# Projecting the low-rank inputs before the shift is known, and adding the shift's nine columns afterwards

## The chip, the cores and the metric

The kernel runs on one core of a Trainium2 chip. The metric is the device time of one execution in microseconds: 1757.57 us, the median of three runs (1754.29 to 1759.15). The five engines are named as the profile names them: PE (TensorE, with PEld for its weight loads), DVE (VectorE), ACT (ScalarE), POOL (GpSimd) and SP (SyncE), which issues nearly all DMA transfers.

## The reference, cut to what matters

One layer of an encoder is computed for 384 tokens: 128 sample tokens (8 sequences of 16) and 256 tokens of one prompt. Only its beginning is touched here.

```python
mod = silu(c) @ w_ada + b_ada              # 9 sequences, 6 x 1024 columns
sh1, sc1, g1, sh2, sc2, g2 = split(mod, 6)
h = rmsnorm(x, norm1_w) * (1 + sc1) + sh1  # sc1, sh1: one row per sequence
P = h @ w_in                               # split into P_rw, P_dsa, P_gate
X = P_rw + (P_prev - P_rw) * mu_rw         # P_prev: the token before
r, k, v, wd, ad, gd = split(X, [1024, 1024, 1024, 64, 64, 160])
w_log = -softplus(-(w0 + tanh(wd) @ w_up)) - 0.5
a = sigmoid(a0 + ad @ a_up)
g = sigmoid(gd) @ g_up
```

The low-rank inputs are the last 288 columns of the RWKV part of `w_in`: wd, ad and gd.

## The kernel before

**Layout.** Activations are kept transposed: `xT` holds 8 chunks of 128 features by 384 tokens, tokens 0 to 127 being the sample. A projection takes its weights as high and low halves (an fp32r copy by ACT, L230, and the remainder by DVE, L234) and the activations likewise (`LTh`, `LTl`). Each chunk then needs three products of 128x384: high x high, low x high, high x low. `tposp` adds 24 of them into one PSUM bank.

**The front, in program order.** `front_x` loads x in three tiles of 128 tokens, normalises them and transposes them into `xT`. `front_h` walks over four pairs of feature chunks. For each pair it calls `mod_unit` twice: a unit loads 256 columns of `w_ada` as two tiles of 512 KB (L240), multiplies them with the nine conditioning rows (products `mm<-w,cst`), copies the result out (`mr`, L391) and turns it into columns with two tiny products (`bx<-cfirst,mr`); DVE adds the bias into `scT` (L396). Units 0 to 3 are the shift, units 4 to 7 the scale. Before, they come in the order 0, 4, 1, 5, 2, 6, 3, 7. Then `h1A` (scale times norm weight) is formed, `xT` is multiplied and shifted, and `LTh` and `LTl` of the pair are written.

**After the front.** `shifted("wa")`, `shifted("wb")` and `shifted("wg")` in `rwkv_head` project the low-rank inputs (units of 128, 128 and 96 columns of `w_in`) with `tposp`, copy them into `pt` and mix each token with the token before it. Then the string `ORDER` sets the sequence of all further units: it starts with two gate units G0 and G1 and the indexer, and goes on with gate units, RWKV pairs, attention quarters and the other 16 modulation units.

**What sets the order of the work.** Nothing is placed by hand at this place. Each engine runs its instructions strictly in the order that the compiler's scheduler gave it, and waits where an input is missing. All 512 KB weight tiles, of `w_ada` and `w_in` alike, share one ring `w` of four buffers (`raw`, L240): SP can ask for the next tile only when the instructions that read the tile four places earlier are done, and everything behind it in SP's queue waits with it. `issue_after` puts what is written in its block behind a named instruction. PSUM has eight banks in rings by tag: `mm` 2, `fx` 2, `dx` 2, `bx` 1, `cp` 1.

**Names around the change.** `tile_pool` objects are regions of SBUF: `ph` serves the front and is given back after it; `rw` and `idx` are opened later, in part on the same memory; `fconst` lives until the end of the RWKV part. `cfront` is a block of constants of 463 KB; DVE builds `expb` (L332) from it, POOL builds the rotary tables `rt` (L341 to L350) from `crope`.

Of the kernel before, what the change touches and what calls it, by code (L numbers as in the profile page):

```python
# [12 lines left out]
F32 = mybir.dt.float32  # L13
# [182 lines left out]
class K:  # L196
# [184 lines left out]
    def mod_unit(self, u):  # L381
# [5 lines left out]
        for h in (first, 1 - first):  # L387
            for g in range(4):
                self.mm(p[32 * g:32 * g + 32], self.st[:, h * 4 + g], w[h][:, g], start=(h == first), stop=(h != first), tp=(0, 32 * g))
        mr = self.t([128, 256], tag="mr", bufs=2, pool=self.fill)  # L390
        nc.scalar.activation(mr, p, AF.Copy)  # L391
        if u < 8:
            q = self.ps([128, 2, 9], tag="bx")
            for c in range(2):
                self.mm(q[:, c], mr[:, c * 128:(c + 1) * 128], self.c["sel"])
            nc.vector.tensor_tensor(self.scT[:, u // 4, (u % 4) * 2:(u % 4) * 2 + 2], q,  # L396
                                    self.bcol[:, 2 * u:2 * u + 2].unsqueeze(2).to_broadcast([128, 2, 9]), op=OP.add)
        else:
            nc.sync.dma_start(self.modd[:, u * 256:(u + 1) * 256], mr)

    def mod_cols(self, cs):
# [42 lines left out]
    def front_x(self):  # L444
# [3 lines left out]
        for i in range(3):  # L448
            x = self.t([128, 1024], tag="x", bufs=2)
            nc.sync.dma_start(x, self.I["x"][i * 128:(i + 1) * 128])  # L450
# [11 lines left out]
    def front_h(self):  # L462
# [6 lines left out]
        self.h1A = self.pool.tile([128, 8, 9], F32, name="h1A")  # L469
        h = self.xT  # L470
        for c in range(0, 8, 2):
            cs = slice(c, c + 2)
            self.mod_unit(c // 2)
            self.mod_unit(c // 2 + 4)
            self.mod_cols(cs)
            hs = h[:, cs, 0:128]
            o = hs.rearrange("p c (b t) -> p c b t", t=16)
            bc = lambda a: a[:, cs, :8].unsqueeze(3).to_broadcast([128, 2, 8, 16])
            nc.vector.tensor_tensor(o, o, bc(self.h1A), op=OP.mult)
            nc.vector.tensor_tensor(o, o, bc(self.h1B), op=OP.add)  # L480
            for cc in (c, c + 1):
# [4 lines left out]
            nc.vector.tensor_tensor(lo[:, cs, 0:128], hs, hi[:, cs, 0:128], op=OP.subtract)  # L486
            nc.gpsimd.tensor_tensor(lo[:, cs, 128:NT], h[:, cs, 128:NT], hi[:, cs, 128:NT], op=OP.subtract)  # L487


    def shifted(self, name, ch, tag, bufs=2):  # L490

        nc = self.nc
        W, m = self.win(name)
        pt = self.t([128, 393], tag="pt", bufs=2)
# [4 lines left out]
        nc.gpsimd.memset(ptp[:, 0:1], 0.0)  # L499
        p = self.tposp(W, 0, m, self.LT)  # L500
        nc.scalar.activation(pts[:, :, 1:], p[:, 0:128].rearrange("p (b t) -> p b t", t=16), AF.Copy)
        nc.scalar.activation(ptp[:, 1:], p[:, 128:NT], AF.Copy)
        Xs = X[:m, 0:128].rearrange("p (b t) -> p b t", t=16)
# [1092 lines left out]
    def run(self):  # L1596
        hs = self.ctx.enter_context(ExitStack())
        self.halves = self.open(hs, "halves")
        with ExitStack() as front:
# [6 lines left out]
            with ExitStack() as s:  # L1606
                self.pool = self.open(s, "ph")
                self.setup()
                self.mod_head()
                self.front_x()  # L1610
                self.front_h()

                self.early = {name: self.raw(self.win_ap(name)) for name in ("wa", "wb", "wg")}
                with self.tc.issue_after(self.wdma.ins):
                    self.load_consts("cfront", self.fconst)
                    self.setup_front()
# [145 lines left out]
```

## Time and profile before

| What | Value |
|---|---|
| three runs | 1754.29, 1757.57, 1759.15 us |
| profiled execution: time, span | 1749.86 us, 1748.1 us |
| busy share of the span | PE 96%, PEld 81%, DVE 78%, ACT 43%, POOL 32% |
| mean granted TensorE clock | 0.983 |
| chain of waits, by engine | PE 61%, DVE 18%, DMA 11%, issue 5%, ACT 3%, POOL 2% |
| PE idle in 0 to 60 us, from the windows view (60 less 43.85 busy) | 16.2 us |
| first product of a modulation unit | 10.96 us |
| first product of the low-rank inputs (wa) | 37.25 us |
| first product of wg | 50.26 us |
| first product of gate unit G0 | 54.54 us |

A row of the timeline reads: start in us, duration in us, engine, source line, operation, output tile <- input tiles, shape, count, and in brackets the idle time of the engine just before and what released it. A row of the windows view reads: stretch, its length, busy us of PE, PEld, DVE, ACT and POOL (with counts of instructions), the granted clock, the busy share of the DMA engines and GB/s. Rows of single products overlap, since matmuls are pipelined: the distance between two starts is what a product costs in a stream.

### The profile page before, as it was taken

How to read it: one execution, taken by the hardware profiler on the slowest of the kernel's cores; microseconds unless marked ns; L12 is line 12 of the kernel's file. 1: busy time of each engine (PE TensorE's matmuls, PEld its weight loads, DVE VectorE, ACT ScalarE, POOL GpSimd, SP SyncE). 2: the span in 40 equal slices, each digit the busy share in tenths (PEclk: the TensorE clock that was granted, in tenths of full speed). 3: DMA queues.
4: the chain of work that ended last, by engine and by line, in shares of the span. 5: the costliest groups of instructions: out<-in, count | busy, mean ns of one | idle time of the engine just before them, and what ended most of it. 6: DMA issues, size and time to landing. Idle time of an engine off the chain costs nothing.

```text
span 1748.1 us, 33136 instructions
## 1 busy us (share of the span) xinstructions
PE 1673.2 (96%) x12392; PEld 1410.4 (81%) x12392; DVE 1356.0 (78%) x2907; ACT 749.5 (43%) x1668; POOL 556.0 (32%) x621
## 2 busy tenths in 40 slices
PE   6999999999999988999998999999999999999998
PEld 4998788888878876999887899999966666767766
DVE  4448788878858855565999998999858777778787
ACT  4443333333343333444323365577843343343344
POOL 2434243343323310034032223431243324433242
PEclk8999899999999999999999999999999999999999
DMA  8543653465365366756398989986579999999996
GB/s 299 166 145 94 198 176 89 144 179 156 103 201 158 95 209 200 243 184 200 123 361 307 364 324 399 397 321 228 170 261 388 347 342 377 366 350 385 348 379 227
DMA packets 173049, 437.23 MB, mean 250 GB/s; under 512 B 46036, under 2 KB 86612, under 8 KB 156504
## 3 DMA queue, kind: packets, MB, share of 16 engines
q1 hardware_dynamic: 154456, 300.89, 50.8%
q0 software_dynamic: 18432, 134.23, 20.0%
q8 instruction: 98, 1.61, 0.4%
q14 instruction: 63, 0.52, 0.1%
HBM read 403.75 MB, written 31.30 MB: 249 GB/s over the span
## 4 chain that ended last, share of the span: by engine, by line
PE 61%; DVE 18%; DMA 11%; issue 5%; ACT 3%; POOL 2%; SPq 0%; DVEq 0%; POOLq 0%; ACTq 0%
PE mm L226 24%; PE fx L226 11%; PE dx L226 11%; PE cp L226 7%; PE bx L226 6%; DMA w<-in_pv 3%; DVE raw L1586 3%; DVE wl L234 3%; DVE acc L1592 3%; DMA raw<-in_puv,pe 2%; DMA w<-in_puT 1%; ACT wh L230 1%; DMA w<-in_w_in 1%; DMA w<-in_w_ada 1%; DVE psi L1321 1%
## 5 line engine op out<-in xcount | busy, mean ns | idle before, releaser
L234 DVE TENSOR_TENSOR wl<-w,wh 128x1024 fp32r<-128x1024 f32 (+1 forms) x276 | 346.9, 1264 | 116.5 <-ACT wh L230 78.4
L230 ACT ACTIVATE wh<-w 128x1024 fp32r<-128x1024 f32 (+1 forms) x284 | 297.0, 1051 | 167.2 <-PE mm L226 68.3
L1579 POOL DMA_INDIRECT raw<-in_puv,pe x128 | 175.5, 1371 | 419.8 <-PE dx L226 160.4
L226 PE MATMUL fx<-h2h,wl 128*128 128x256 f32 x704 | 199.6, 284 | 4.7 <-DVE wl L234 4.6
L226 PE MATMUL fx<-h2h,wh 128*128 128x256 f32 x704 | 200.7, 285 | 3.3 <-ACT wh L230 1.7
L226 PE MATMUL fx<-h2l,wh 128*128 128x256 f32 x704 | 197.3, 280 | 0.0
L1592 DVE SCALAR_TENSOR_TENSOR acc<-raw,dots,acc 128x1024 f32<-128x1024 f32 x127 | 166.1, 1308 | 13.7 <-ACT dots L1588 13.6
L1586 DVE SCALAR_TENSOR_TENSOR raw<-raw,sh 128x1024 f32<-128x1024 f32 x128 | 158.6, 1239 | 12.3 <-DMA raw<-in_puv,pe 12.2
L226 PEld LDWEIGHTS fx<-h2h,wh 128*128 128x128 f32 x704 | 132.8, 189 | 7.9 <-ACT wh L230 3.9
L226 PEld LDWEIGHTS fx<-h2h,wl 128*128 128x128 f32 x704 | 132.6, 189 | 7.9 <-DVE wl L234 7.1
L226 PEld LDWEIGHTS fx<-h2l,wh 128*128 128x128 f32 x704 | 132.9, 189 | 1.6 <-issue 1.1
L226 PE MATMUL mm<-LTh,wh 128*128 128x384 f32 (+2 forms) x352 | 124.0, 353 | 1.8 <-ACT wh L230 1.2
L226 PE MATMUL mm<-LTl,wh 128*128 128x384 f32 (+2 forms) x352 | 122.2, 347 | 1.2 <-POOL LTl L487 1.2
L226 PE MATMUL mm<-LTh,wl 128*128 128x384 f32 (+2 forms) x352 | 122.6, 348 | 0.0
L226 PE MATMUL mm<-h2f,w 128*128 128x256 f32 x448 | 105.5, 389 | 0.0
L226 PE MATMUL mm<-wh,LTh 128*128 128x256 f32 x336 | 99.3, 296 | 0.8 <-ACT qx L890 0.6
L226 PE MATMUL mm<-wl,LTh 128*128 128x256 f32 x336 | 100.0, 298 | 0.0
L226 PE MATMUL mm<-wh,LTl 128*128 128x256 f32 x336 | 98.8, 294 | 0.0
L1587 ACT ACTIVATE dots<-dots 128x1 f32<-128x1 f32 x128 | 25.5, 200 | 169.8 <-DVE raw L1586 169.2
L226 PEld LDWEIGHTS mm<-h2f,w 128*128 128x128 f32 x448 | 86.2, 195 | 12.6 <-issue 0.2
L226 PE MATMUL fx<-h2f,w 128*128 128x256 f32 x320 | 73.5, 382 | 0.0
L226 PEld LDWEIGHTS mm<-LTh,wh 128*128 128x128 f32 (+2 forms) x352 | 66.5, 189 | 7.3 <-ACT wh L230 2.1
(583 smaller groups left out, 4241.8 us busy)
## 6 DMA issues: line engine op xcount, KB each, us to landing
w<-in_puT SPq DMA_DIRECT2D x128, 512.0 KB, 6.2
w<-in_pv SPq DMA_DIRECT2D x128, 512.0 KB, 6.7
w<-in_w_in SPq DMA_DIRECT2D x70, 512.0 KB, 4.7
w<-in_w_ada SPq DMA_DIRECT2D x48, 512.0 KB, 4.9
cKT<-in_cKT SPq DMA_DIRECT2D x32, 256.0 KB, 4.4
cV<-in_cV SPq DMA_DIRECT2D x32, 256.0 KB, 4.0
w<-in_w_pq SPq DMA_DIRECT2D x16, 512.0 KB, 3.8
d<-wst SPq DMA_DIRECT2D x8, 832.0 KB, 4.3
```

The costliest lines, as they stand in the source:

```text
L226: return self.nc.tensor.matmul(out, l, r, start=start, stop=stop, skip_group_check=True, **kw)
L230: self.nc.scalar.activation(hi, src, AF.Copy)
L234: (self.nc.vector if eng == "v" else self.nc.gpsimd).tensor_tensor(lo, src, hi, op=OP.subtract)
L1321: nc.vector.max_index(si[:, half, h, 0:8], sv[:, half, h, 0:8], s[:, c])
L1579: d = nc.gpsimd.indirect_dma_start(out=bass.AP(tensor=u.tensor, offset=u.offset, ap=[u.ap[0], [1, 2048]]), out_offset=None, in_=self.I["puv"],
L1586: nc.vector.scalar_tensor_tensor(u, u, 1.0, h2, op0=OP.mult, op1=OP.mult, accum_out=dot)
L1587: nc.scalar.activation(dot, dot, AF.Gelu_apprx_tanh)
L1592: nc.vector.scalar_tensor_tensor(acc, v, dot, acc, op0=OP.mult, op1=OP.add)
```

## The change

1. `front_h` now runs the four scale units first (4, 5, 6, 7) and the four shift units after them (0, 1, 2, 3).
2. The low-rank weights wa, wb and wg get tiles of their own instead of places in the ring. They are loaded and split into halves behind the first scale unit, so ahead of 14 of the 16 tiles of `w_ada`.
3. After each scale unit the pair of chunks of x times scale is written as halves `EPh` and `EPl` (three ACT and three DVE instructions per pair), and the products of wa and wb with this pair are added into two `dx` banks. The 24 products of wg go into the `cp` bank, all behind the last product of the last shift unit.
4. After the last shift unit the nine shift columns are copied into a zeroed tile `z` (32 columns wide) and projected with the raw weights: 24 products into 32-row strips of a bank, one copy out (`shm`) and three small products that give `eshift` (128 x 9 for each of the three units).
5. `shifted` then reads the three banks directly and adds `eshift`: one DVE addition with a broadcast for the sample tokens, one ACT copy with a bias for the prompt.
6. `x` has three buffers instead of two; `shT` moves to another pool and is loaded ahead of `cfront`; the two ring places that were loaded ahead for wa and wb now hold G0 and G1.

```diff
@@ mod_unit
-                self.mm(p[32 * g:32 * g + 32], self.st[:, h * 4 + g], ...)
+                last = self.mm(p[32 * g:32 * g + 32], self.st[:, h * 4 + g], ...)
...
+        return last
@@ front_x
-            x = self.t([128, 1024], tag="x", bufs=2)
+            x = self.t([128, 1024], tag="x", bufs=3)
@@ front_h
+        eh, el = (self.t([128, 8, NT], F32R, tag=x) for x in ("EPh", "EPl"))
+        z = self.t([128, 8, 32], tag="shz")
+        nc.gpsimd.memset(z, 0.0)
+        names = ("wa", "wb", "wg")
+        self.ebank, W = {}, {}
+
+        def products(n, ks):
+            wh, wl, m, _ = W[n]
+            p = self.ebank[n][:m]
+            for k in ks:
+                self.mm(p, wh[:, k], eh[:, k], start=(k == 0), stop=False)
+                self.mm(p, wh[:, k], el[:, k], start=False, stop=False)
+                self.mm(p, wl[:, k], eh[:, k], start=False, stop=(k == 7))
+
         for c in range(0, 8, 2):
             cs = slice(c, c + 2)
-            self.mod_unit(c // 2)
             self.mod_unit(c // 2 + 4)
             self.mod_cols(cs)
+            if c == 0:
+                for n, tag in zip(names, ("dx", "dx", "cp")):
+                    m = UNITS[n][1]
+                    w = self.t([128, 8, m], tag=n)
+                    nc.sync.dma_start(w, self.win_ap(n))
+                    wh, wl = (self.t([128, 8, m], F32R, tag=n + x) for x in "hl")
+                    self.hilo(wh, wl, w)
+                    W[n] = wh, wl, m, w
+                    self.ebank[n] = self.ps([128, NT], tag=tag)
             hs = h[:, cs, 0:128]
             o = hs.rearrange("p c (b t) -> p c b t", t=16)
-            bc = lambda a: a[:, cs, :8].unsqueeze(3).to_broadcast([128, 2, 8, 16])
-            nc.vector.tensor_tensor(o, o, bc(self.h1A), op=OP.mult)
-            nc.vector.tensor_tensor(o, o, bc(self.h1B), op=OP.add)
+            nc.vector.tensor_tensor(o, o, self.h1A[:, cs, :8]..., op=OP.mult)
+            nc.scalar.activation(eh[:, cs, 0:128], hs, AF.Copy)
+            nc.vector.tensor_tensor(el[:, cs, 0:128], hs, eh[:, cs, 0:128], op=OP.subtract)
+            for cc in (c, c + 1):
+                hp, A = h[:, cc, 128:NT], self.h1A[:, cc, 8:9]
+                nc.scalar.activation(eh[:, cc, 128:NT], hp, AF.Identity, scale=A, bias=0.0)
+                nc.vector.scalar_tensor_tensor(el[:, cc, 128:NT], hp, A, eh[:, cc, 128:NT], ...)
+            for n in names[:2]:
+                products(n, (c, c + 1))
+        for c in range(0, 8, 2):
+            cs = slice(c, c + 2)
+            last = self.mod_unit(c // 2)
+            hs = h[:, cs, 0:128]
+            nc.vector.tensor_tensor(o, o, self.h1B[:, cs, :8]..., op=OP.add)
...
-
+        with self.tc.issue_after(last.ins):
+            products(names[2], range(8))
+
+        nc.vector.tensor_copy(z[:, :, 0:9], self.h1B)
+        p = self.ps([128, 352], tag="mm")
+        q = self.ps([128, 3, 9], tag="bx")
...
+        for i, n in enumerate(names):
+            _, _, m, w = W[n]
+            for h2 in range(2):
+                for g in range(4):
+                    k = h2 * 4 + g
+                    self.mm(p[32 * g:32 * g + 32, i * 128:i * 128 + m], z[:, k], w[:, k],
+                            start=(h2 == 0), stop=(h2 == 1), tp=(0, 32 * g))
+        nc.scalar.activation(mr, p, AF.Copy)
+        for i, n in enumerate(names):
+            m = W[n][2]
+            self.mm(q[:m, i], mr[:, i * 128:i * 128 + m], self.c["sel"])
+            nc.vector.tensor_copy(self.eshift[:m, i], q[:m, i])
@@ shifted
+        if early:
+            p, B = self.ebank[name][:m], self.eshift[:m, ch - 24]
+            nc.vector.tensor_tensor(pts[:, :, 1:], p[:, 0:128]..., B[:, 0:8]..., op=OP.add)
+            nc.scalar.activation(ptp[:, 1:], p[:, 128:NT], AF.Identity, scale=1.0, bias=B[:, 8:9])
@@ run
-                self.early = {name: self.raw(self.win_ap(name)) for name in ("wa", "wb", "wg")}
+                self.early = {name: self.raw(self.win_ap(name)) for name in ("G0", "G1")}
                 with self.tc.issue_after(self.wdma.ins):
+                    self.shT = self.fconst.tile([128, 8, 27], F32, name="shT")
+                    self.nc.sync.dma_start(self.shT, self.I["shT"])
```

Three places of the new order matter below. On PE, in the middle of the modulation units (`mm<-w,cst` are a unit's products, four to a row, `bx` its columns; `mm_277` is unit 6, `mm_316` unit 7 and `mm_355` unit 0 of the change). Before:

```order
L226 MATMUL mm_268<-w_269,cst 32x256 x4
L226 MATMUL mm_268<-w_271,cst 32x256 x4
L226 MATMUL mm_287<-w_288,cst 32x256 x4
L226 MATMUL bx_283<-cfirst,mr_281 128x9 x2
L226 MATMUL mm_287<-w_290,cst 32x256 x4
L226 MATMUL mm_315<-w_316,cst 32x256 x4
L226 MATMUL bx_302<-cfirst,mr_300 128x9 x2
L226 MATMUL mm_315<-w_318,cst 32x256 x4
```

Now:

```order
L226 MATMUL dx_211<-EPh_174,wbl_208 128x384
L226 MATMUL mm_277<-w_278,cst 32x256 x4
L226 MATMUL bx_253<-cfirst,mr_251 128x9 x2
L226 MATMUL mm_277<-w_280,cst 32x256 x4
L226 MATMUL mm_316<-w_317,cst 32x256 x4
L226 MATMUL mm_316<-w_319,cst 32x256 x4
L226 MATMUL bx_292<-cfirst,mr_290 128x9 x2
L226 MATMUL dx_204<-EPh_174,wah_200 128x384
L226 MATMUL dx_211<-EPh_174,wbh_207 128x384
L226 MATMUL mm_355<-w_356,cst 32x256 x4
L226 MATMUL dx_204<-EPl_175,wah_200 128x384
L226 MATMUL dx_204<-EPh_174,wal_201 128x384
```

Groups of twelve low-rank products (`dx`), one group for each pair of chunks, now stand between the halves of the units; the first row shown ends the first group, the eighth begins the second. Two products of the first group and two of the second stand ahead of a half of unit 5 and of unit 0.

On PE, where the low-rank products end and G0 begins (`mm_561` before, `mm_627` now). Before:

```order
L226 MATMUL mm_506<-LTh_171,wh_498 96x384
L226 MATMUL mm_506<-LTl_172,wh_498 96x384
L226 MATMUL mm_506<-LTh_171,wl_499 96x384
L226 MATMUL mm_561<-LTh_171,wh_556 128x384
L226 MATMUL mm_561<-LTl_172,wh_556 128x384
```

Now:

```order
L226 MATMUL cp_218<-EPh_174,wgl_215 96x384
L226 MATMUL bx_448<-cfirst,mr_446 128x9 x2
L226 MATMUL mm_484<-wa_198,shz_176 32x128 x8
L226 MATMUL mm_484<-wb_205,shz_176 32x128 x8
L226 MATMUL mm_484<-wg_212,shz_176 32x96 x8
L226 MATMUL mm_627<-LTh_171,wh_622 128x384
L226 MATMUL mm_627<-LTl_172,wh_622 128x384
```

Between the last product of wg and the first of G0 there now stand the columns of the last shift unit and the 24 shift products, which read `z`.

On DVE, around the last unit's columns (`scT<-bx_448`, before `scT<-bx_349`). Before:

```order
L396 TENSOR_TENSOR scT<-bx_349,bcol 128x18
L234 TENSOR_TENSOR wl_499<-w_366,wh_498 128x768
L332 TENSOR_TENSOR expb<-cfront 128x512
L1064 TENSOR_SCALAR ob_350_1816<-cfront 128x8
L403 SCALAR_TENSOR_TENSOR h1A<-scT,cols 128x18
```

Now:

```order
L234 TENSOR_TENSOR wl_656<-w_521,wh_655 128x1024
L515 TENSOR_TENSOR xT_107<-xT_107,scT 128x2x128
L332 TENSOR_TENSOR expb<-cfront 128x512
L1126 TENSOR_SCALAR ob_355_1880<-cfront 128x8
L520 CAST LTh_171<-xT_107 128x2x256
L396 TENSOR_TENSOR scT<-bx_448,bcol 128x18
L521 TENSOR_TENSOR LTl_172<-xT_107,LTh_171 128x2x128
L515 TENSOR_TENSOR xT_107<-xT_107,scT 128x2x128
L526 COPY shz_176<-scT 128x8x9
```

`expb`, which needs `cfront`, stood behind the last `scT` and now stands ahead of it; `shz` is the copy into `z` that the shift products read.

More of the change, by code (lines that the diff above doesn't have):

```diff
@@ L388, in mod_unit @@
             for g in range(4):
-                self.mm(p[32 * g:32 * g + 32], self.st[:, h * 4 + g], w[h][:, g], start=(h == first), stop=(h != first), tp=(0, 32 * g))
+                last = self.mm(p[32 * g:32 * g + 32], self.st[:, h * 4 + g], w[h][:, g], start=(h == first), stop=(h != first), tp=(0, 32 * g))
         mr = self.t([128, 256], tag="mr", bufs=2, pool=self.fill)
@@ L476, in front_h @@
             hs = h[:, cs, 0:128]
             o = hs.rearrange("p c (b t) -> p c b t", t=16)
-            bc = lambda a: a[:, cs, :8].unsqueeze(3).to_broadcast([128, 2, 8, 16])
-            nc.vector.tensor_tensor(o, o, bc(self.h1A), op=OP.mult)
-            nc.vector.tensor_tensor(o, o, bc(self.h1B), op=OP.add)
+            nc.vector.tensor_tensor(o, o, self.h1A[:, cs, :8].unsqueeze(3).to_broadcast([128, 2, 8, 16]), op=OP.mult)
+            nc.scalar.activation(eh[:, cs, 0:128], hs, AF.Copy)
+            nc.vector.tensor_tensor(el[:, cs, 0:128], hs, eh[:, cs, 0:128], op=OP.subtract)
@@ new lines, in front_h @@
+            for cc in (c, c + 1):
+                hp, A = h[:, cc, 128:NT], self.h1A[:, cc, 8:9]
+                nc.scalar.activation(eh[:, cc, 128:NT], hp, AF.Identity, scale=A, bias=0.0)
+                nc.vector.scalar_tensor_tensor(el[:, cc, 128:NT], hp, A, eh[:, cc, 128:NT], op0=OP.mult, op1=OP.subtract)
+            for n in names[:2]:
[4 more added lines that the diff above has]
+            hs = h[:, cs, 0:128]
+            o = hs.rearrange("p c (b t) -> p c b t", t=16)
+            nc.vector.tensor_tensor(o, o, self.h1B[:, cs, :8].unsqueeze(3).to_broadcast([128, 2, 8, 16]), op=OP.add)
@@ L487, in front_h @@
             nc.gpsimd.tensor_tensor(lo[:, cs, 128:NT], h[:, cs, 128:NT], hi[:, cs, 128:NT], op=OP.subtract)
+        with self.tc.issue_after(last.ins):
[3 more added lines that the diff above has]
+        q = self.ps([128, 3, 9], tag="bx")
+        mr = self.t([128, 352], tag="shm")
+        self.eshift = self.fconst.tile([128, 3, 9], F32, name="eshift")
+        for i, n in enumerate(names):
[10 more added lines that the diff above has]
+            nc.vector.tensor_copy(self.eshift[:m, i], q[:m, i])
     def shifted(self, name, ch, tag, bufs=2):
         nc = self.nc
-        W, m = self.win(name)
+        early = name in self.ebank
+        if early:
+            m = UNITS[name][1]
+        else:
+            W, m = self.win(name)
         pt = self.t([128, 393], tag="pt", bufs=2)
@@ L499, in shifted @@
         nc.gpsimd.memset(ptp[:, 0:1], 0.0)
-        p = self.tposp(W, 0, m, self.LT)
-        nc.scalar.activation(pts[:, :, 1:], p[:, 0:128].rearrange("p (b t) -> p b t", t=16), AF.Copy)
-        nc.scalar.activation(ptp[:, 1:], p[:, 128:NT], AF.Copy)
+        if early:
+            p, B = self.ebank[name][:m], self.eshift[:m, ch - 24]
+            nc.vector.tensor_tensor(pts[:, :, 1:], p[:, 0:128].rearrange("p (b t) -> p b t", t=16),
+                                    B[:, 0:8].unsqueeze(2).to_broadcast([m, 8, 16]), op=OP.add)
+            nc.scalar.activation(ptp[:, 1:], p[:, 128:NT], AF.Identity, scale=1.0, bias=B[:, 8:9])
+        else:
+            p = self.tposp(W, 0, m, self.LT)
+            nc.scalar.activation(pts[:, :, 1:], p[:, 0:128].rearrange("p (b t) -> p b t", t=16), AF.Copy)
+            nc.scalar.activation(ptp[:, 1:], p[:, 128:NT], AF.Copy)
         Xs = X[:m, 0:128].rearrange("p (b t) -> p b t", t=16)
```

2 lines of the change are left out of this document (removed).

## The prediction, as it was put on record

> **What bounds the kernel now.** I read the page first, then the stretches of the front, then its timeline row by row, and last what SP waits for.
>
> ```profile
> span 1748.1 us, 33136 instructions
> PE 1673.2 (96%) x12392; PEld 1410.4 (81%) x12392; DVE 1356.0 (78%) x2907; ACT 749.5 (43%) x1668; POOL 556.0 (32%) x621
> 0.00:10.00 10.00, 0.93 (x5) 0.94 (x6) 3.18 (x14) 3.84 (x6) 4.65 (x10) 1.00 0.71 250
> 10.00:20.00 10.00, 9.37 (x85) 5.61 (x83) 2.70 (x8) 5.62 (x11) 0.55 (x1) 1.00 0.99 350
> 20.00:30.00 10.00, 6.58 (x56) 3.04 (x60) 3.08 (x10) 3.43 (x10) 2.77 (x2) 0.72 0.91 310
> 30.00:40.00 10.00, 8.73 (x50) 5.33 (x50) 5.74 (x10) 4.65 (x9) 1.27 (x1) 0.50 0.93 326
> 60.00:70.00 10.00, 10.00 (x63) 9.21 (x62) 6.59 (x11) 7.11 (x12) 1.16 (x4) 1.00 0.62 186
> 100.00:120.00 20.00, 20.00 (x113) 18.68 (x112) 6.54 (x16) 7.29 (x14) 2.79 (x8) 1.00 0.56 166
> 140.00:160.00 20.00, 20.00 (x145) 18.90 (x144) 19.98 (x58) 7.41 (x17) 10.22 (x18) 1.00 0.39 115
> ```
>
> PE is busy 96% of the span, so the kernel as a whole is PE's. From 60 to 160 us it has no gap at all, so whatever PE gains or loses by the time G0 starts arrives at 160 us unchanged. The front is different: from 20 to 40 us the DMA engines are over 90% busy at 310 to 326 GB/s, PE has gaps, and its clock is granted at half. The quantity to forecast is therefore when G0's first product runs. Before, that is at 54.54:
>
> ```profile
> 16.73 0.61 PE L226 MATMUL bx<-cfirst,mr 128*128 128x9 f32 x4
> 18.90 1.07 PE L226 MATMUL mm<-w,cst 128*32 128x256 f32 x16
> 28.73 2.23 PE L226 MATMUL mm<-w,cst 128*32 128x256 f32 x16
> 33.96 1.02 PE L226 MATMUL bx<-cfirst,mr 128*128 128x9 f32 x4
> 34.92 1.08 PE L226 MATMUL mm<-w,cst 128*32 128x256 f32 x8
> 40.83 0.52 PE L226 MATMUL mm<-LTh,wl 128*128 128x384 f32 x1
> 41.15 0.49 PE L226 MATMUL mm<-LTh,wh 128*128 128x384 f32 x1
> 43.90 0.34 PE L226 MATMUL mm<-LTh,wh 128*128 128x384 f32 x1
> 44.07 0.34 PE L226 MATMUL mm<-LTl,wh 128*128 128x384 f32 x1
> 47.66 0.44 PE L226 MATMUL mm<-LTl,wh 128*128 128x384 f32 x1 [1.17 <-POOL LTl L487]
> 50.26 0.42 PE L226 MATMUL mm<-LTh,wh 128*96 128x384 f32 x1 [0.59 <-ACT pt L502]
> 54.54 0.34 PE L226 MATMUL mm<-LTh,wh 128*128 128x384 f32 x1
> ```
>
> A unit (two halves) takes 1.07 us at full clock and 2.23 at half, its columns (two products, four instructions) 0.61 and 1.02. A low-rank product costs 0.32 us at half clock (40.83 to 41.15) and 0.17 at full (43.90 to 44.07). The last unit's half starts at 34.92. The low-rank stage then runs until 54.54: from 37.25 (the table above) that is 17.3 us for 72 products, which at 0.17 are 12.3 us. Half clock until after 41.15 and two waits, 1.17 and 0.59, are the rest. At most this stage can be hidden; the question is what it pushes back.
>
> **The change part by part.**
>
> *More loads ahead of the modulation.* wa, wb and wg (512, 512 and 384 KB, 1.44 MB) go ahead of 14 halves of `w_ada`. At 326 GB/s that is 4.4 us. If SP always has a free buffer to fill, the last half arrives 4.4 us later and its products start at 39.3.
>
> *The ring is now emptied more slowly.* SP waits for PE:
>
> ```profile
> SPq L240 <- PE mm L226: 16.8, 13, 2.6
> w<-in_w_ada SPq DMA_DIRECT2D x16, 512.0 KB, 5.2
> 19.54 1.09 ACT L483 ACTIVATE xT<-xT,scT,h1A 128x256 f32<-128x256 f32 x2
> 20.52 0.41 ACT L484 ACTIVATE LTh<-xT 128x256 fp32r<-128x256 f32 x1
> 36.14 1.06 ACT L230 ACTIVATE wh<-w 128x1024 fp32r<-128x1024 f32 x1 [2.09 <-DMA w<-in_w_in]
> 39.68 0.84 ACT L230 ACTIVATE wh<-w 128x768 fp32r<-128x768 f32 x1 [1.20 <-DMA w<-in_w_in]
> ```
>
> In the new order the first twelve `dx` products stand ahead of unit 6 and wait for `EPh`. ACT reaches `EPh` behind the splits of all three low-rank weights. What is asked for up to wg is 4.2 MB (x 1.57, two halves 1.05, the three 1.44, small ones 0.17); at 250 GB/s until 10 us and 350 after it has moved at 14.9 us, 16.5 with its landing. Then ACT still owes, of its queue, about 2 us of earlier work, 0.84 for wg's split and 1.5 for the first `EPh`: PE starts the group near 20. Twelve products at half clock are 3.8 us and the half unit among them 1.1: unit 6 begins at 25, and only then, near 26, does its first buffer come free for unit 0's first half, which lands 5.2 us later, at 31.2. Seven halves follow at 1.6 us each (524 KB at 326 GB/s): the last lands at 42.4. At full clock throughout it would be 39.5. I take 42.4, since the clock of this stretch was 0.72 on average and falling, and keep 39.3 as the low bound.
>
> *From the last half to G0.*
>
> ```profile
> 35.49 0.16 DVE L396 TENSOR_TENSOR scT<-bx,bcol 128x18 f32<-128x18 f32 x1
> 32.84 0.43 DVE L480 TENSOR_TENSOR xT<-xT,scT 128x256 f32<-128x256 f32 x1
> 33.51 0.43 DVE L485 CAST LTh<-xT 128x512 fp32r<-128x512 f32 x1 [0.24 <-ACT xT L483]
> 34.46 0.42 SPq L297 DMA_DIRECT2D cfront<-in_cfront  x1
> 41.43 0.75 DVE L332 TENSOR_TENSOR expb<-cfront 128x512 bf16<-128x512 f32 x1
> 42.96 3.43 POOL L350 TENSOR_TENSOR rt<-rt,qkn 128x96 f32<-128x96 f32 x8
> ```
>
> The half itself: 0.8 us (0.54 to 1.1). The 24 products of wg follow at once: 4.1 us at 0.17, 7.7 at 0.32; I take 5, because between units the array had gone slow before. The last columns: 0.8. So the last `scT` can be formed at 49.0. Here the new order adds a wait: DVE has put `expb` ahead of it, whose `cfront` took 7.0 us from its request to its use before (34.46 to 41.43). It is now asked for behind G0 and G1, whose buffers come free near 40.5, so it is there at about 48. Then DVE runs `expb` 0.75, a small one 0.23, the cast 0.43, `scT` 0.16, a remainder 0.43, the shift of `xT` 0.43 and the copy 0.2. That ends at 50.7, about 1.7 us after PE is done with the columns. Queued behind on PE are the shift products and then G0, though G0's first thirteen products need nothing from them.
>
> *The 24 shift products* have no row of their kind. From below: 16 instructions of a 256-column unit take 1.07, so 48 of 128 columns or fewer take at least 1.4 at full clock; from above, 3 x 1.08 = 3.2 at half clock if each group cost what a half unit costs. I take 2.1, nearer to the unit's row. Three small products like those of `bx`, 0.3 to 0.5 each by its rows, come later in G0's stream: 0.9.
>
> *Sum:* 42.4 + 0.8 + 5 + 0.8 + 1.7 + 2.1 = 52.8, and 0.9 in the stream makes 53.7, against 54.54: a gain of 0.8 us. A wait of almost 2 us ahead of the shift products endangers the clock:
>
> ```profile
> 166.00:169.00 3.00, 1.86 (x18) 1.35 (x16) 2.01 (x15) 0.49 (x1) 0.31 (x1) 1.00 0.12 11
> 169.00:172.00 3.00, 2.21 (x9) 1.52 (x10) 3.00 (x12) 1.43 (x4) 1.09 (x1) 0.86 0.00 0
> 172.00:175.00 3.00, 2.86 (x11) 2.13 (x10) 3.00 (x8) 1.71 (x4) 1.88 (x2) 0.50 0.08 22
> ```
>
> Idle times of 1.14 and 0.79 us in neighbouring stretches were enough there to halve it, and in the front dense products had it back only between 41.15 and 43.90. I charge 0 to 1.7 us for that (some eleven G0 products at 0.32 instead of 0.17), 0.8 in the sum: change 0.0 us. [...]
>
> *What costs nothing.* The additional ACT and DVE work of the scale units lies beside transfers (busy 3.1 and 3.4 of 10 us from 20 to 30). POOL's tables (3.43 us of `rt` among them) now stand between its `LTl` pieces, but G0's first thirteen products need only the first two; if PE came early, at 47, the last piece would hold it back, as it did for 1.17 us at 47.66. `XD` and `XW` come later and their products now stand some 100 products further back; the first RWKV pair is not needed on PE until 129.47 (its `fx<-cfront,sq`):
>
> ```profile
> 129.47 0.73 PE L226 MATMUL fx<-cfront,sq 128*128 128x2 f32 x6
> 58.70 0.81 PE L226 MATMUL fx<-XD,wup 128*128 128x384 f32 x2
> ```
>
> That is 70 us of cover. Without it the 15 us that they move would be added in part.
>
> **The rivals.**
>
> *The front is hidden as named (faster).* The last half starts at 39.3, everything runs at full clock, and DVE is not late: 39.3 + 0.6 + 4.1 + 0.6 + 1.3 + 1.4 = 47.3, and 0.9: gain 6.3 us. For it: DMA was over 90% busy, so the products would really fill PE's waits. Against it: the order itself empties the ring late, and 0.50 was granted for all of 30 to 40. Time: 1751.3.
>
> *Half clock while PE feeds the ring (slower).* If the second group of twelve runs at 0.32 too, it costs 1.8 us more, and one more unit with its columns 1.6 (2.23 + 1.02 against 1.07 + 0.61): the last half starts 3.4 us later. wg at 7.7 adds 2.7 to the 5, and the full charge on G0's first products 0.9: 7.0 us slower, 1765. It decides from the point at which the second group still costs over 0.3 us a product. For it: units and columns alone, with PE 97 to 100% busy from 28 to 36, did not raise the clock. Against it: dense products did.
>
> *The rest of the program is rearranged.* Behind the front the scheduler chose other orders between RWKV pairs and attention quarters. Two transfers that PE's chain waits for there show the price:
>
> ```profile
> 628.80 7.34 DMA w<-in_w_ada
> 660.40 5.97 DMA w<-in_w_proj_a
> ```
>
> A request placed elsewhere in SP's queue can remove or double one of them: 1751 or 1764. The sequence of units is the same in both, so I give this little.
>
> *The products do not overlap with the loads* (the change does not do what it says) would need ACT to reach `EPh` only after the scale units; the order excludes it.
>
> **How the numbers follow.** The sum is made against the profiled execution (span 1748.1, 1.8 us around it: 1749.86), which lies 7.7 us under the median of the runs; a change of 0 puts the median at 1757.6, and I say 1758. From no change this kernel's runs tell about 0.3%, 5.3 us. Chances: no change 0.50 (its own range, 1753 to 1763), hidden front 0.18, half clock 0.20, rearrangement 0.12 (0.05 faster, 0.07 slower). Faster 0.23, same 0.50, slower 0.27. Both outer cases belong to the range: 1750 to 1766.
>
> **What would show it.** Right: the ring's requests (`w<-in_w_ada`) near 26 us waiting for PE; the last unit's half near 42; PE idle 1 to 3 us between `bx` and the shift products with DVE's copy as the releaser; G0's first product within 3 us of 54.5; no gap from there to 160. The first rival shows as G0 near 47 to 48. The second as `dx` products 0.32 apart beyond 33 us. The third as a G0 near 54 with a total that moved all the same. My forecast fails if G0's start and the total part by more than 5 us, or if the group of twelve does not delay unit 6.

## The result and the profile after

The change made the kernel slower: 1780.69 us, the median of six runs (1775.65 to 1783.81), against 1756.42 (1750.02 to 1762.71) for the kernel before. The ratio is 1.0138, 95% interval 1.0119 to 1.0158. That is 24 us; the forecast was no change, and 1766 its upper end. The profiled execution took 1783.81 us. That lies 3.1 us above its median, and the profiled execution of the kernel before (1749.86) lies 6.6 us below its own, so the two traces are 34 us apart.

The head of the page of the changed kernel:

```profile
span 1782.0 us, 33233 instructions
PE 1695.0 (95%) x12446; PEld 1425.3 (80%) x12446; DVE 1364.0 (77%) x2926; ACT 753.9 (42%) x1678; POOL 551.3 (31%) x622
```

Its timeline of PE in the front:

```profile
19.47 0.44 PE L226 MATMUL dx<-EPh,wah 128*128 128x384 f32 x1 [2.19 <-ACT EPh L506]
...
24.04 0.64 PE L226 MATMUL mm<-w,cst 128*32 128x256 f32 x8
...
40.49 1.49 PE L226 MATMUL mm<-w,cst 128*32 128x256 f32 x20
...
46.91 0.58 PE L226 MATMUL bx<-cfirst,mr 128*128 128x9 f32 x4
...
51.68 1.08 PE L226 MATMUL mm<-wa,shz 128*32 128x128 f32 x16 [4.18 <-DVE shz L526]
...
54.18 0.69 PE L226 MATMUL mm<-LTh,wh 128*128 128x384 f32 x1
```

The front does what was forecast: the first `dx` group at 19.5, unit 6 at 24.0, the last unit's second half at the end of the row that starts at 40.49, G0's first product at 54.18 (54.54 before). The total moved all the same. To see where, I followed SP's requests in both traces. These are `w_ada` tiles of M8 (the ninth unit) and M12, and then the tile of G7. Before:

```profile
148.63 0.33 SPq L240 DMA_DIRECT2D w<-in_w_ada  x1
...
260.54 0.33 SPq L240 DMA_DIRECT2D w<-in_w_ada  x1
...
336.66 0.33 SPq L240 DMA_DIRECT2D w<-in_w_in  x1
```

After:

```profile
153.45 0.33 SPq L240 DMA_DIRECT2D w<-in_w_ada  x1
...
263.89 0.33 SPq L240 DMA_DIRECT2D w<-in_w_ada  x1
...
361.82 0.33 SPq L240 DMA_DIRECT2D w<-in_w_in  x1
```

M8 is 4.8 us late, M12 3.4, G7 25.2. Two places lose time: some 5 us between G0 and 149 us, and some 22 us between 264 and 362. The other 9 of the 34 us come behind G7 and were not followed; the places of the two executions in their own scatter (3.1 and 6.6 us) are as large. The first stretch is no gapless stretch any more. The changed kernel's windows there, and the row of PE's timeline that ends the hole:

```profile
75.00:80.00 5.00, 3.21 (x20) 2.76 (x19) 4.30 (x9) 2.70 (x7) 2.26 (x7) 0.87 0.15 38
80.00:90.00 10.00, 10.00 (x77) 9.93 (x77) 6.67 (x6) 5.74 (x11) 6.77 (x6) 0.89 0.35 105
```

```profile
77.24 0.39 PE L226 MATMUL mm<-wh,LTh 128*128 128x256 f32 x1 [1.79 <-ACT qx L952]
```

The second in windows, before:

```profile
300.00:310.00 10.00, 9.23 (x146) 8.50 (x145) 9.36 (x22) 1.42 (x4) 5.40 (x8) 1.00 0.40 102
310.00:320.00 10.00, 10.00 (x110) 9.41 (x109) 8.72 (x18) 4.71 (x8) 4.84 (x4) 1.00 0.60 182
320.00:330.00 10.00, 9.17 (x90) 7.68 (x90) 8.94 (x16) 1.66 (x5) 8.23 (x8) 0.91 0.07 18
```

and after:

```profile
300.00:310.00 10.00, 7.63 (x67) 6.15 (x65) 9.18 (x28) 5.05 (x14) 3.84 (x5) 0.87 0.03 8
310.00:320.00 10.00, 10.00 (x117) 9.22 (x115) 5.06 (x16) 0.00 (x0) 1.40 (x4) 0.50 0.29 61
320.00:330.00 10.00, 9.87 (x86) 8.49 (x82) 8.12 (x19) 2.09 (x6) 3.93 (x7) 0.61 0.36 114
```

PE has a hole of 2.37 us, and from within it on 20 us at half clock (0.50 in the window from 307.39 to 327.87, 1.00 just before and behind it), although behind the hole it is busy nearly all the time (19.66 of these 20.48 us). The hole stands ahead of the second RWKV pair's `cp<-S,TT`. PE there, before and after:

```profile
298.27 0.28 PE L226 MATMUL mm<-wl,LTh 128*128 128x256 f32 x1
298.38 0.29 PE L226 MATMUL mm<-wh,LTl 128*128 128x256 f32 x1
298.60 1.09 PE L226 MATMUL cp<-S,TT 64*64 64x128 f32 x16
```

```profile
305.43 0.28 PE L226 MATMUL mm<-wh,LTl 128*128 128x256 f32 x1
308.08 1.97 PE L226 MATMUL cp<-S,TT 64*64 64x128 f32 x16 [2.37 <-ACT S L816]
```

Both read ACT's copy `S`, but before PE did not have to wait for it: `S` was done at 296.62. Between `fx<-cfront,sq` and these products thirteen projection products of the attention quarter stood before, one each 0.12 us (the last two are shown); in the new order four are left. The nine that are gone would fill about 1.1 us, by an estimate from these 0.12 us; the rest of the hole is that `S` comes late. ACT too has another order: `S` now comes behind `sig`, which waits for DVE.

```profile
307.02 0.53 ACT L629 ACTIVATE sig<-sig 128x384 f32<-128x384 f32 x1 [0.39 <-DVE sig L628]
307.45 0.58 ACT L816 ACTIVATE S<-cp 128x512 f32<-128x512 f32 x1
```

And in the 22 us behind it the pair's small dependent products have no such company. The projection's products (tile `mm`) alone, before and after:

```profile
299.00:321.00 22.00, 10.75 (x76) 1.00 0.47 131
```

```profile
308.00:330.00 22.00, 0.83 (x5) 0.55 0.30 80
```

So the theory to test was **O**: the time is lost because the scheduler, given another front, arranged the pairs and quarters behind it in another order (1624 of the 4408 PE instructions from the first gate unit to the mixing leave their place, by the two order tables of e1 and e2 below). Its rival **F**: the new front itself costs it, through what it leaves behind. A third candidate is the late start of the low-rank head at about 65 us.

### The profile page after: what moved, and what is told of

It reads as the page before. It is cut to its first block, busy times and chain, and to the rows that moved or that the text cites. A ratio compares the mean times of both kernels' runs of the same rounds, so it can differ in the third digit from the quotient of the medians.

```text
span 1782.0 us, 33233 instructions
## 1 busy us (share of the span) xinstructions
PE 1695.0 (95%) x12446; PEld 1425.3 (80%) x12446; DVE 1364.0 (77%) x2926; ACT 753.9 (42%) x1678; POOL 551.3 (31%) x622
## 3 DMA queue, kind: packets, MB, share of 16 engines
q0 software_dynamic: 18432, 134.23, 19.5%
## 4 chain that ended last, share of the span: by engine, by line
PE 56%; DVE 20%; DMA 12%; issue 6%; ACT 3%; POOL 2%; SPq 1%; DVEq 0%; POOLq 0%; ACTq 0%
PE mm L226 21%; PE fx L226 11%; PE dx L226 10%; PE cp L226 6%; PE bx L226 6%; DMA w<-in_pv 4%; DVE wl L234 3%; DVE raw L1648 3%; DMA raw<-in_puv,pe 2%; DVE acc L1654 2%; DMA w<-in_puT 2%; ACT wh L230 1%; DMA d<-MBp 1%; DVE TX L762 1%; DMA NL<-d 1%
## 5 line engine op out<-in xcount | busy, mean ns | idle before, releaser
L234 DVE TENSOR_TENSOR wl<-w,wh 128x1024 fp32r<-128x1024 f32 x273 | 343.2, 1265 | 104.6 <-ACT wh L230 71.0
L230 ACT ACTIVATE wh<-w 128x1024 fp32r<-128x1024 f32 x281 | 294.0, 1053 | 158.9 <-PE mm L226 73.1
L226 PE MATMUL mm<-LTh,wh 128*128 128x384 f32 (+1 forms) x328 | 115.0, 351 | 0.0
L226 PE MATMUL mm<-LTh,wl 128*128 128x384 f32 (+1 forms) x328 | 114.6, 349 | 0.4 <-DVE wl L234 0.4
L226 PE MATMUL mm<-LTl,wh 128*128 128x384 f32 (+1 forms) x328 | 112.8, 344 | 0.0
L1649 ACT ACTIVATE dots<-dots 128x1 f32<-128x1 f32 x128 | 25.7, 201 | 185.0 <-DVE raw L1648 184.5
L226 PEld LDWEIGHTS mm<-wh,LTh 128*128 128x128 f32 x336 | 65.5, 195 | 6.0 <-ACT qx L952 3.5
```

The lines of the kernel that those rows point to most:

```text
L226: return self.nc.tensor.matmul(out, l, r, start=start, stop=stop, skip_group_check=True, **kw)
L230: self.nc.scalar.activation(hi, src, AF.Copy)
L234: (self.nc.vector if eng == "v" else self.nc.gpsimd).tensor_tensor(lo, src, hi, op=OP.subtract)
L1649: nc.scalar.activation(dot, dot, AF.Gelu_apprx_tanh)
```

## The experiments

### The order alone: e1, e2, e3

The order of a kernel can be carried over: the ranks in which another kernel's instructions are issued, for each engine, are put into a table, and an edge without a wait between neighbours fixes them.

```diff
+ORDER_OF = ...
+def pin(tc, start):
...
+    for e, ranks in want.items():
+        for a, b in zip(ranks, ranks[1:]):
+            tc.add_manual_dep(by[e][b], by[e][a].name, mybir.DependencyInfo(
+                mybir.DependencyClass.NoSync, mybir.DependencyReason.DATA), reason="pin")
```

What fixing an order costs by itself was not run alone. The nearest is e9 below, where the kernel before keeps its own order by such a table, with some products added: 1.0019.

> The changed kernel, with the instructions behind the low-rank head (RWKV pairs, attention quarters, gates, modulation units up to the mixing) issued on every engine in the order that they had before the change; the new front stays. The edges fix the order only and add no wait. Theory O (the new order of the middle costs the time): the front ended level with the old one (G0 at 54.18 against 54.54), so the total falls back to that of the kernel before, ratio 0.997 to 1.003, and the weight requests of r4 to V2 come no more than 3 us later than before (they came up to 33 us later). Theory F (the new front costs it, through what it leaves behind in memory, queues and clock): it stays near 1.0138. Mixed: the 5 to 6 us lost by 160 us belong to the front, the later 20 to the order: 1.003 to 1.004.

> The kernel before, its front untouched, with the same stretch issued in the changed kernel's order. Theory O: it becomes as slow as the change, ratio 1.010 to 1.016, with the loss between the requests of r4 and V2. Theory F: ratio 0.997 to 1.003. Mixed: 1.009 to 1.012, since the loss before 160 us stays away.

e3 changes the kernel before only so:

```diff
                 with self.tc.issue_after(self.wdma.ins):
+                    self.shT = self.fconst.tile([128, 8, 27], F32, name="shT")
+                    self.nc.sync.dma_start(self.shT, self.I["shT"])
                     self.load_consts("cfront", self.fconst)
...
-        self.shT = self.t([128, 8, 27], tag="shT")
-        nc.sync.dma_start(self.shT, self.I["shT"])
```

> The kernel before with one small part of the change: the shift state shT (one transfer of 108 KB) is asked for ahead of cfront and lies in the front's constants, instead of in the low-rank head. The front's products are as before. The scheduler answers with a third order of the middle: 1197 of its 4408 PE instructions leave their place in the old sequence, from the same point on (PE's 831st instruction of the middle) as in the change. If any such new order costs about what the change's does, ratio 1.008 to 1.016; if it is that one order alone that is bad, 0.997 to 1.003; if orders scatter to both sides, anything from 0.992 to 1.008. By theory F, which asks for the new front, 0.997 to 1.003.

Measured: e1 1.008 (1.0053 to 1.0106), e2 1.0115 (1.0072 to 1.0157), e3 0.9998 (0.9975 to 1.0021). The old front with the new order loses most of what the change loses: theory F cannot explain that. A third order costs nothing, so it is not rearrangement as such. e1 came out between the theories, and its trace shows why: the old order was also forced on the seam, where G0 now waits for its split weights and the first pair's transforms for a copy.

```profile
57.37 0.69 PE L226 MATMUL mm<-LTh,wl 128*128 128x384 f32 x1 [2.59 <-DVE wl L234]
...
65.08 0.88 PE L226 MATMUL fx<-XD,wup 128*128 128x384 f32 x2 [1.70 <-POOL pt L557]
```

### Seam, late head and front: e4 to e7

e4 is e1 with the table starting at the products of ki. e5 is the change with this edit, e6 both together, and e7 is e6 with two waits of the front mended.

```diff
             self.mm(q[:m, i], mr[:, i * 128:i * 128 + m], self.c["sel"])
-            nc.vector.tensor_copy(self.eshift[:m, i], q[:m, i])
+        nc.vector.tensor_copy(self.eshift[:, 0:2], q[:, 0:2])
+        nc.vector.tensor_copy(self.eshift[:96, 2], q[:96, 2])
```

> As the first run, but the old order is kept only from the products of ki on; G0, G1 and the low-rank head stay as the change has them. In the first run the old order also covered the seam: it put G0's second half, and the transforms XD and XW, where the new front has them late, and PE stood 2.59 us for wl and 1.70 us for pt between 54 and 65 us, which cost 7 us by the requests of G4. Theory O with a front's share: that 7 us go, the 5 us that the change itself lost by 80 us (PE's 1.79 us for qx and half clock from 79.0 to 82.4) stay; ratio 1.001 to 1.005. If the order is worth only the 0.006 between the change and the first run: 1.007 to 1.009.

> The changed kernel, but the three small products of eshift stand together and are read by two copies behind them, instead of a copy behind each, with which the scheduler spread them through G0 and G1 (56.85, 60.60, 63.47 us), so that the low-rank head's chain on DVE, ACT and POOL began at 64.89 us instead of 51. The middle's order stays the changed one (12 of 4408 PE instructions leave their place). If the late eshift is what the front costs: the head begins 7 us earlier, PE's wait for qx near 77 us and the half clock behind it go, the requests of r0 to V1 come 0 to 2 us later than in the kernel before instead of 5 to 6, ratio 1.009 to 1.012. If it costs nothing: 1.012 to 1.016. If the loss at 300 to 350 us was set off by the lateness and not by the order: 1.000 to 1.004.

> Both: eshift's products together, and the old order from ki on. If order and late eshift are the two causes and nothing else is: ratio 0.998 to 1.002. If something else of the front costs (its loads, the larger pool): 1.003 or more.

> The run before this one in the list with two waits of the front mended too: on DVE the copy to z is issued ahead of expb and of G1's split, and G0's first twelve products are issued on PE ahead of the shift products (whose sums take a bank of fx instead of one of mm). In the changed kernel PE stood 4.18 us for z from 47.5 to 51.7 and had half clock from 51.7 to 55.1. If these cost what they show, some 3 to 5 us are gained on the run before it: ratio 0.995 to 0.999, the first chance to be faster than the kernel before. If PE's time there is hidden or given back in the waits behind: as the run before it, 0.998 to 1.002.

| | changed order | old order from ki |
|---|---|---|
| change | 1.0138 (1.0119 to 1.0158) | e4 1.0057 (1.0038 to 1.0076) |
| eshift together | e5 1.012 (1.0077 to 1.0163) | e6 1.004 (1.0014 to 1.0065) |
| front mended too | | e7 1.0033 (1.001 to 1.0056) |

Across a row the order is worth 0.8%, 14 us, twice. Down a column the late `eshift` is worth 0.2%, 3 us, which the intervals do not separate from nothing. The traces show where it comes from. DVE's copies of `eshift` in the change, and in e5:

```profile
57.18 0.17 DVE L542 COPY eshift<-bx 128x9 f32<-128x9 f32 x1 [2.99 <-PE bx L226]
...
61.47 0.16 DVE L542 COPY eshift<-bx 128x9 f32<-128x9 f32 x1
...
64.81 0.15 DVE L542 COPY eshift<-bx 96x9 f32<-96x9 f32 x1
```

```profile
56.08 0.18 DVE L542 COPY eshift<-bx 128x18 f32<-128x18 f32 x1 [3.04 <-PE bx L226]
56.17 0.15 DVE L543 COPY eshift<-bx 96x9 f32<-96x9 f32 x1
```

In the change the small products share one bank, each has its copy behind it, and the scheduler spread them through G0 and G1. The head then ran beside the indexer. On ACT the copy `qx`, for which PE stood 1.79 us, comes behind a copy of the head (`XVh`) that waits for DVE. In the change:

```profile
76.39 0.53 ACT L230 ACTIVATE XVh<-sig 128x384 fp32r<-128x384 f32 x1 [1.77 <-DVE sig L442]
76.82 0.64 ACT L952 ACTIVATE qx<-mm 128x256 f32<-128x256 f32 x2
```

In e5 PE waits 0.50 us there, and SP's requests of M8, M12 and G7 stand so:

```profile
148.73 0.33 SPq L240 DMA_DIRECT2D w<-in_w_ada  x1
...
257.36 0.33 SPq L240 DMA_DIRECT2D w<-in_w_ada  x1
...
355.58 0.33 SPq L240 DMA_DIRECT2D w<-in_w_in  x1
```

M8 is level with the kernel before (148.63), M12 ahead by 3 us, and G7 again 19 us late. From M12 to G7 the order's stretch costs what it did: 98.2 us here, 97.9 in the change, 76.1 before. M12's lead belongs to the order too: e2, with the old front, asks for it at 258.22, 2.3 us ahead.

That M8 is level does not mean that the front is neutral. G0's start differs between executions, so the stretch behind it has to be read from there:

| | G0's first product | request of M8 | between |
|---|---|---|---|
| before | 54.54 | 148.63 | 94.1 |
| change | 54.18 | 153.45 | 99.3 |
| e4 | 51.74 | 150.99 | 99.3 |
| e5 | 51.72 | 148.73 | 97.0 |
| e6 | 54.20 | 150.90 | 96.7 |

The late `eshift` is worth 2.3 us (the change against e5) and 2.6 us (e4 against e6), as the ratios have it. With `eshift` mended 2.6 to 2.9 us remain between G0 and M8; e5 hides them because its G0 came 2.8 us before that of the kernel before. What they consist of was not priced. e7 did not gain: PE's wait for z fell from 4.18 to 0.58 us, but it stood 2.5 us for `pt` and 1.5 us for `gg` behind it.

### Is it the clock: e15, e8, e9, e10

e2's times lay far apart (1761.0 to 1776.56), and the profiled one was the fastest. e15 is the same kernel once more.

> The kernel of the second run (old front, the changed kernel's order) once more, for another trace. Profiled there: 1761.0 us, 3.4 us at half clock between 300 and 345 us; its other executions took 1767.0 to 1776.6. If the long stretch at half clock makes the difference: an execution of 1767 us or more shows 10 to 25 us of half clock between 300 and 345, one of 1761 to 1764 shows 0 to 7. If the difference lies elsewhere: a slow execution with no more than 7 us of half clock there.

It took 1774.48 us. The windows of 300 to 340 us in e2, and in e15:

```profile
300.00:340.00 40.00, 34.83 (x429) 29.55 (x428) 31.58 (x90) 11.23 (x25) 12.33 (x16) 0.96 0.33 92
```

```profile
300.00:340.00 40.00, 38.63 (x367) 32.74 (x367) 25.64 (x68) 8.95 (x20) 10.56 (x15) 0.66 0.27 73
```

PE's hole ahead of the second pair, and G7's request, in e2 and then in e15:

```profile
300.99 1.09 PE L226 MATMUL cp<-S,TT 64*64 64x128 f32 x16 [0.80 <-ACT S L754]
...
348.38 0.33 SPq L240 DMA_DIRECT2D w<-in_w_in  x1
```

```profile
301.24 1.40 PE L226 MATMUL cp<-S,TT 64*64 64x128 f32 x16 [1.32 <-ACT S L754]
...
355.16 0.33 SPq L240 DMA_DIRECT2D w<-in_w_in  x1
```

One program, level at 300 us to a quarter of a microsecond. Where the hole was 0.80 us the clock was 1.00 from 300 to 310 us and 0.83 from 310 to 320, some 3.4 us at half; where it was 1.32 us the clock was at half for 27 of the 40 us from 300 on (1 less 0.66, twice, of 40), and G7 came 6.8 us later. The holes end a quarter of a microsecond apart (300.99 and 301.24), and their lengths differ by 0.52. It is one pair of executions; whether the length alone makes the difference was not shown. By this pair the price of the order has two parts: its holes and unaccompanied small products, 12 us at G7 nearly without the clock (348.38 against 336.66), and the long half clock that the stretch fell into in one of the two, 7 us more there and 13.5 in the total of these two executions.

That PE was busy again did not bring the full clock back at once here. In the change PE is busy, as the profile counts it, for 10.00 of 10 us from 310 to 320, with products of 32 to 128 columns, at 0.50, and the clock is back at 327.9. In e15 it is busy for 9.87 of 10 us from 310 to 320 at 0.50, and for 10.00 from 320 to 330 at 0.54.

The other runs of this group fill PE's holes with products whose sums nobody reads. The core of e8's edit:

```diff
+        if e == 1:
+            self.fill_pe("chain", 12, self.ps([128, NT], tag="cs"))
         p = self.ps([128, 2, 2, 128], tag="cp")
```

> The changed kernel in its own order, with twelve additional products (128x384, 0.17 us each, 2.0 us in all, their sums never read) on PE ahead of the second pair's cp<-S,TT, where PE stood 2.37 us (305.97 to 308.35) for ACT's copy S and the clock was at half from 307.7 to 328.1. The wait itself stays, only its idleness goes. If the half clock behind that hole is what makes the order dear: no half clock there, up to 10 us (half of 20.4) gone, ratio 1.007 to 1.010. If the clock falls anyway, or PE there waits for DVE and ACT and not for its own clock: 1.012 to 1.015.

> The run with eshift's products together, in its own order (the changed one), with the same twelve products ahead of the second pair's cp<-S,TT, where PE stood 2.25 us (299.43 to 301.68) and the clock was at half for 20.5 of the 23 us behind it and for 10 more from 331. If the half clock is the order's price: from 1.012 to 1.004 to 1.007. If not: 1.011 to 1.013.

> The kernel before in its own order, with products of that kind in three of its holes: 8 ahead of the first pair's fx<-cfirst,Xk (PE idle 1.68 us at 168.1), 18 ahead of the first quarter's dx<-cfirst,qr (3.41 us at 190.8), 24 of 256 columns (0.12 us each) ahead of the modulation unit that waits 3.11 us for w_ada at 633.4. Half clock stood behind these from 171.4 to 178.3, 195.3 to 202.2 and 635.7 to 642.5, 20.5 us together. If holes cost twice, by themselves and by the clock behind them: up to 10 us gone, ratio 0.994 to 0.998. If the clock there hides in other waits: 0.999 to 1.001. If the holes lie elsewhere in other executions, so that the products stand in PE's way: 1.001 to 1.003.

e8: 1.0113 (1.0093 to 1.0133), e10: 1.0107 (1.0086 to 1.0128). e8 lies between what was expected of the one theory and of the other, e10 at the edge of the second, and neither is clear of the kernel without the filling (1.0138 and 1.012; the intervals overlap). e8's windows behind the filled hole show why:

```profile
300.00:310.00 10.00, 10.00 (x131) 8.84 (x131) 9.39 (x27) 4.03 (x10) 2.59 (x5) 1.00 0.17 38
310.00:320.00 10.00, 8.38 (x117) 7.14 (x113) 9.47 (x28) 1.40 (x4) 3.10 (x5) 0.78 0.33 90
320.00:330.00 10.00, 10.00 (x66) 8.49 (x63) 6.33 (x16) 2.17 (x5) 3.77 (x4) 0.54 0.21 62
```

The hole is gone, but 8 us later PE has smaller ones in the same stretch (0.65 us of waiting for DVE's `Sb`, up to 315.06; 8.38 of 10 us busy from 310 to 320), and from 310 to 330 the clock is at half for 13.6 us (0.78 and 0.54). Here one filled hole did not mend a stretch that has several.

e9: 1.0019 (1.0002 to 1.0036), so no gain where half a per cent was hoped for; it lies in the range that was expected if the products stand in PE's way in other executions. The windows, and the last request ahead of M12, before and in e9:

```profile
160.00:225.00 65.00, 59.26 (x459) 47.74 (x459) 52.33 (x155) 25.24 (x52) 18.78 (x23) 0.89 0.59 175
...
250.16 0.33 SPq L240 DMA_DIRECT2D w<-in_w_in  x1
```

```profile
160.00:225.00 65.00, 62.97 (x526) 53.08 (x525) 54.52 (x162) 25.88 (x54) 20.99 (x26) 0.97 0.59 179
...
248.74 0.33 SPq L241 DMA_DIRECT2D w<-in_w_in  x1
```

The clock rose from 0.89 to 0.97, which is 5 us of the full clock, but the request comes only 1.4 us earlier, and that is lost again later. In the kernel before PE waits there 3.4 us for DVE's `qr` and 1.7 us for its `MKp`. That PE at the higher clock only waited longer there is how I read it; no run separates this from products that stand in the way.

### Other orders: e11 to e14

e11 puts e3's order behind e5's front. In e12 to e14 the scheduler finds its own order to a front that differs in a detail from e5's; e12's edit is

```diff
-                    self.setup_front()
+                    with self.tc.issue_after(self.zc.ins):
+                        self.setup_front()
```

e13 asks for `cfront`, `shT` and the tables ahead of G0's weights, and e14 is e7's front without a table.

> The new front with eshift's products together, and behind ki the third order, which on the old front gave 0.9998. If the new front with eshift mended costs nothing by itself: 0.998 to 1.002. If 0.4% belong to the front: 1.003 to 1.005. If an order is only good for the front it was made for: anything up to 1.008.

> The new front with eshift's products together and one edge more: on DVE the tables of the front (expb and the identity's sum) are issued behind the copy to z. Nothing behind the front is held to an order. The scheduler answers with an order near the third one: 481 of 4408 PE instructions stand elsewhere than in it, 1284 elsewhere than in the changed one, 1093 elsewhere than in the old one. If the order is what counts: 0.998 to 1.003, although the front is the changed one. If the front costs 0.8% or more: 1.008 to 1.012.

> The new front with eshift's products together; cfront, shT and the tables are asked for ahead of G0's and G1's weights instead of behind them. Again the scheduler finds its own order, a fifth one, far from all others (1693 of 4408 PE instructions stand elsewhere than in the changed one, 1615 elsewhere than in the old one). Nothing tells beforehand where it lies: if orders scatter, 0.998 to 1.012, with the loss or gain between the requests of M12 and G7; G0 and G1 come about 2 us later by themselves.

> The mended front of the seventh run (copy to z first on DVE, twelve products of G0 ahead of the shift products) with the order that the scheduler finds for it, a sixth one. The mended front with the old order gave 1.0033. If that remainder is the mismatch of front and order, this one can lie at 0.996 to 1.003; if this order has holes of its own, up to 1.012.

| | ratio | mean clock, 300 to 340 us |
|---|---|---|
| e11 | 1.0024 (1.0004 to 1.0044) | 1.00 |
| e13 | 1.0051 (1.0029 to 1.0073) | 1.00 |
| e12 | 1.012 (1.0084 to 1.0157) | 0.61 |
| e14 | 1.0182 (1.0148 to 1.0215) | 1.00, but 0.60 from 600 to 630 |

The rows of e12 and of e14:

```profile
300.00:340.00 40.00, 36.70 (x306) 31.27 (x303) 29.44 (x77) 9.81 (x26) 9.96 (x15) 0.61 0.19 51
```

```profile
600.00:630.00 30.00, 26.03 (x207) 20.85 (x206) 15.85 (x34) 4.84 (x15) 6.99 (x11) 0.60 0.18 42
```

Of e11's twelve executions one took 9172.45 us; the ratio goes by the other eleven (1755.28 to 1765.23). The orders scatter from 1.002 to 1.018 on nearly the same front. e12's order is close to the third one, which had cost nothing, and it still cost 1.2%: likeness of the sequences told nothing here. The profiled executions over 1770 us have a mean clock of 0.61 to 0.79 from 300 to 340 us (the change 0.74, e5 0.63, e10 0.79, e12 0.61, e15 0.66), which is 17 to 31 us at half, or, in e14, 0.60 from 600 to 630. PE's holes there lie in an RWKV pair: it waits for `S` 2.37 us in the change, 2.25 in e5, 1.27 in e12 and 1.32 in e15, and in e14 twice for a transfer, `TN<-d`, 3.5 us together. Of the profiled executions below 1770 us, e8 (1767.92) has 0.79 from 300 to 340; the other ten have 0.96 or 1.00.

No run beat the kernel before. **What stays open:** the new front was never below 1.0024. The third order cost nothing on the old front (e3, 0.9998) and 0.24% on the new one (e11), with intervals that overlap. Between G0 and M8 the traces with `eshift` together (e5, e6, e10, e11) take 96.7 to 97.7 us against 94.1 before; that is about 3 us, or 0.15 to 0.2%, on the side of the front. Whether the rest of the last 0.2 to 0.4% belongs to the front or to orders that do not fit it is not settled.

## Why the prediction was wrong

**Right, in part by luck: the front.** The ring emptied late as worked out (unit 6 forecast at 25, came at 24.04), wg's products took 5.0 us as taken, and G0 started 0.4 us earlier than before, where no change was forecast. That the start agrees so closely is luck: six other traces with the same front up to there (e4, e5, e6, e8, e10, e11) start G0 between 51.65 and 54.20.

**Terms of the sum were mis-sized, and the errors nearly cancelled.** The wait for DVE, taken as 1.7 us, measured 4.18: besides `expb`, G1's split (1.23 us) and an earlier pair's `xT` (0.48) stood ahead of the last `scT`, as the new order had shown. The shift products measured 2.50 us (51.68 to 54.18) against 2.1. Against these 2.9 us the last columns were done 1.5 us sooner than summed (47.49 against 49.0), so G0 came 1.4 us behind the 52.8 of the sum; the 0.9 and 0.8 us that were added to 52.8 for what follows G0's start make the total look exact. The clock was at half from 51.4 to 54.8 (0.50 in that window), so the charge for it came under the shift products and not as eleven slow G0 products.

**The first failing step: "From 60 to 160 us it has no gap at all, so whatever PE gains or loses by the time G0 starts arrives at 160 us unchanged".** The stretch is gapless only while all that feeds it is on time. The change delays not G0 but the low-rank head, from 51 to 65 us. The prediction covered its 15 us by the first pair's need at 129 us ("That is 70 us of cover") and looked for the next reader of its results. It should have looked for whom the head's work meets on ACT and DVE: the indexer's copy `qx` stands behind the head's `XVh`. From G0 to M8 the stretch grew by 5.2 us; 2.3 to 2.6 of them are the late `eshift` (e5 and e6 show it), the rest is not assigned. The 0.9 us in G0's stream for the three small products was near as PE time (some 0.7, by the distances of their starts); what they held up behind them was not counted.

**The step that decided: "The sequence of units is the same in both, so I give this little".** The sequence of SP's requests says nothing about where PE's projection products stand beside a pair's chain. The rival was named, and its price was taken from the wrong rows: one transfer wait of 6 to 7 us. The runs put it at 14 us (e4, e6) to 20 us (e2; 17 by its medians), most of it in a place where the kernel before showed nearly no wait at all, since `S` came early there and products stood in between. A table of the products between `fx<-cfront,sq` and `cp<-S,TT`, thirteen before and four after, could have been read from the two orders.

**The sign "a G0 near 54 with a total that moved all the same"** was the right one for this rival, and it is what came.

## What to carry to other kernels

When a scheduler orders the program, an edit in one stage is two edits: the stage, and a new order of everything behind it. Compare the orders where a serial chain is covered by independent products, and count the cover. To measure the stage alone, fix the old order behind it; to judge an order, look for holes ahead of small products and read the clock behind them (0.74 from 300 to 340 us in the change, 0.96 before), and take several executions, since one program gave 0.96 and 1761.0 us in e2 and 0.66 and 1774.48 us in e15. Read the stages from an event that both traces share: here G0's start alone moved by 2.5 us between executions of one front.

## What the runs showed of the hardware

- One program, one place, two executions: with a hole of 1.32 us in front of small products (e15) the mean clock from 300 to 340 us was 0.66, which is 27 us at half; with one of 0.80 us (e2) it was 1.00 from 300 to 310 us and 0.96 from 300 to 340.
- In the change the clock was at half from 307.4 to 327.9 us; from 310 to 320 PE was busy for 10.00 of 10 us, with products of 32 to 128 columns, at 0.50. From 300 to 340 us e8 and e10 show 17 us at half (0.79) and e12 31 us (0.61).
- From 20 to 360 us the clock was at 0.50 in these windows: before, 24.4 to 41.5, 171.2 to 178.0, 195.1 to 201.9 and 328.2 to 331.6 us; in the change, 20.7 to 24.1, 51.4 to 54.8, 78.7 to 82.1, 174.3 to 184.5, 201.6 to 208.4, 307.4 to 327.9 and 348.4 to 351.8 us.
- In e9 the clock rose from 0.89 to 0.97 over the 65 us from 160 on, 5 us of the full clock; the request behind them came 1.4 us earlier, and the ratio was 1.0019. In the kernel before PE waits there 3.4 us for DVE's `qr` and 1.7 us for its `MKp`.
